# The paged compressed cache laid out by page with contraction elements as rows, gathered page by page and split without transposes

## The chip, the cores and the metric

The kernel runs on one core of a Trainium2 chip. The metric is the device time of one execution in microseconds (us). TensorE is called PE, its weight loads PEld; VectorE is DVE, ScalarE ACT, GpSimd POOL, SyncE SP. SP and POOL issue the DMAs: SP's go through the queue that the profile calls hardware_dynamic (q1), POOL's through software_dynamic (q0), and both run on the same 16 DMA engines.

## The reference

One step of a decoder layer on a prompt of 512 tokens and 8 sample sequences of 4 tokens, with D_MODEL 1024. The change is in the compression of the sample sequences' paged past (1024 rows in 8 pages of 128 for each), and in how x, c and the vectors arrive.

```python
def rmsnorm(x, g):
    xf = x.astype(jnp.float32)
    inv = lax.rsqrt(jnp.mean(xf * xf, axis=-1, keepdims=True) + EPS)
    return (xf * inv).astype(x.dtype) * g

def compress(rows, pe, w1, w2):
    b, t, g, d = rows.shape
    nc = t // CMP_STRIDE
    halves = jnp.pad(rows, ((0, 0), (0, CMP_STRIDE), (0, 0), (0, 0))).reshape(b, nc + 1, CMP_STRIDE, g, d)
    blocks = jnp.concatenate([halves[:, :-1], halves[:, 1:]], axis=2) + pe[:, None, :]
    flat = blocks.transpose(0, 1, 3, 2, 4).reshape(b, nc, g, CMP_BLOCK * d)
    return jax.nn.gelu(flat @ w1) @ w2

def nsa_sample(q, gates, kv_cmp, kv_sel, kv_win, cache_cmp, cache_sel, cache_win, page_table, pe, w1, w2, slopes):
    ...
        rows = cache[page_table].reshape(b, past, 2, N_KV, HEAD_DIM)
    ...
    kc, vc = compress_kv(full_rows(cache_cmp, kv_cmp), pe, w1, w2)
    ...
    mod = jax.nn.silu(c) @ w['w_ada'] + w['b_ada']
    h = rmsnorm(x, w['norm1']) * (1 + sc1) + sh1
```

CMP_STRIDE is 16 and CMP_BLOCK 32, so each block of 32 rows (2048 values of one key or value head) is two halves of 16 rows, and each half is used by two blocks. `w1` is 2048 x 128 for keys and again for values, `w2` 128 x 64.

## The kernel before

All products that need precision are made of three matmuls: each operand is split into a high part (ACT, a copy in the type fp32r) and a low part (DVE, the difference), and hi*hi, lo*hi and hi*lo are summed in PSUM (`mm3`, L222 to L224). Weights come as slabs of 1 MB (`slab`, L208, 128 rows of 8 KB, three buffers with the tag `raw`).

The first stage builds the compressed keys and values of the sample sequences. POOL gathers 1 MB at a time from `cache_cmp` by indices made on DVE from the page table (`cmp_gather`, L466; sixteen gathers, two buffers), DVE copies a gather into order (`cmp_copy`, L476), PE transposes its 128 x 128 pieces against the identity so that the contraction lies on partitions (`cmp_T`, L484), ACT and DVE split the PSUM result (L486, L487), and `cmp_M` (L498 to L500) multiplies by the split `w1`: the moving operand is 512 columns wide, the second half of a block is reached by reading one column further (`c0 = lp * 512 + s`), and one PSUM tile sums a pair of sequences over four gathers. `cmp_finish` (L504 to L514) adds the bias, applies gelu and the second layer. Between these run `mod_slab` 0 to 7 (L269, matmuls of silu(c) with slabs of `w_ada`; `mod_fin`, L280), `phi_split` and `phi_bias` (L440, L441, L447), and in the second half `modulate` (L343 to L345), which makes `h` for the input projection.

Before that stage x arrives as rows and is transposed on PE (L545, L549), its squares are summed by ACT along the row, and c, the vectors and the position table come through small DMAs and small transposes (L577, L580, L585).

After the stage the projection's `linear` calls follow (first `kv_type`), then the attention parts and the feed-forward part; at the end of `modulate` x is stored to `x_dr` (L609) and read back much later.

The order of the instructions of each engine is set when the program is built, by a scheduler that follows the order of the code and moves single instructions ahead where their inputs come earlier. Each engine works its list in order; a wait holds back what stands behind it.

```python
        pool.indirect_dma_start(out=t, out_offset=None, in_=ccv, in_offset=bass.IndirectOffsetOnAxis(ap=ixc[:, col:col + 1], axis=0))
...
                pe.transpose(p[:, g * 128:(g + 1) * 128], g2t[lp][:, v * 4 + g].rearrange("p l d -> p (l d)"), ident)
...
                pe.matmul(po, lhsT=w_h, rhs=mh, start=first, stop=False)
                pe.matmul(po, lhsT=w_l, rhs=mh, start=False, stop=False)
                pe.matmul(po, lhsT=w_h, rhs=ml, start=False, stop=last)
```

## Time and profile before

| what | us |
|---|---|
| median of 3 runs (1332.07 to 1332.87) | 1332.23 |
| the profiled execution, its own time | 1332.59 |
| its span, first to last instruction | 1330.8 |
| first `phi` matmul | 20.22 |
| first `lin` matmul (the compression stage ends) | 161.78 |

The span lies inside the profiled execution's time. A group of instructions in the profile is named by line, engine and operation, then output <- input and the shape, the count, the busy time and the mean time of one in ns, and the idle time before them with what ended it. The busy time of a matmul is the time from its start until its result is out; several are under way at once, so the distance from one start to the next says what one costs in a stream.

### The profile page before, as it was taken

Reading aid. Unit: us, or ns where it says so; the run is one execution under the profiler, and the core shown is the slowest. Engines: PE = TensorE matmul, PEld = TensorE weight load, DVE = VectorE, ACT = ScalarE, POOL = GpSimd, SP = SyncE. Lnnn points to the kernel's source line nnn. Section 1 sums busy time; section 2 is a strip of 40 time slices with the busy share of each in tenths; the row PEclk is TensorE's granted clock in tenths of the full one; section 3 lists DMA queues with packets and bytes.
Section 4 is the critical chain, followed back from the end, with each engine's and each line's share of the span. In section 5 each row is a group of like instructions: output and inputs, shape, how many; then the busy total and the mean of one; then the engine's idle time right before and its main releaser. Section 6 shows DMA issues by size and latency. Waiting matters only on the chain.

```text
span 1330.8 us, 25612 instructions
## 1 busy us (share of the span) xinstructions
PE 1306.2 (98%) x10832; PEld 1206.7 (91%) x10832; DVE 652.3 (49%) x1569; ACT 537.9 (40%) x1065; POOL 69.7 (5%) x123
## 2 busy tenths in 40 slices
PE   7999999999999999999999999999999999999997
PEld 5788899999999988998778778999999999999996
DVE  5549332235455454426677586667333333333335
ACT  6335233433233335226677676345332323222223
POOL 2101030000111110001000000000000000000000
PEclk8999999999999999999999999999999999999999
DMA  9896135763545443834546324431113222122211
GB/s 352 295 329 232 40 113 177 279 225 117 197 179 222 165 159 115 221 119 137 134 143 181 125 91 180 137 127 64 64 64 120 71 90 101 57 88 88 88 65 68
DMA packets 35352, 193.56 MB, mean 145 GB/s; under 512 B 4561, under 2 KB 9945, under 8 KB 17702
## 3 DMA queue, kind: packets, MB, share of 16 engines
q1 hardware_dynamic: 30630, 149.98, 33.4%
q0 software_dynamic: 4608, 41.95, 8.3%
q8 instruction: 85, 1.39, 0.4%
q14 instruction: 29, 0.24, 0.1%
HBM read 174.47 MB, written 25.76 MB: 150 GB/s over the span
## 4 chain that ended last, share of the span: by engine, by line
PE 95%; DMA 2%; DVE 1%; ACT 0%; issue 0%; POOL 0%; POOLq 0%; ACTq 0%; DVEq 0%
PE lin L222 19%; PE lin L223 19%; PE lin L224 19%; PE dn L223 3%; PE dn L222 3%; PE dn L224 3%; PE acc L1162 3%; PE ptp L1168 3%; PE phi L500 2%; PE phi L498 2%; PE phi L499 2%; PE xt L484 2%; PE modp L269 2%; PE kt L879 2%; PE sp L1137 1%; PE sp L1138 1%
## 5 line engine op out<-in xcount | busy, mean ns | idle before, releaser
L222 PE MATMUL lin<-h_hi,wh 128*128 128x288 f32 (+1 forms) x1648 | 478.5, 291 | 0.0
L223 PE MATMUL lin<-h_lo,wh 128*128 128x288 f32 (+1 forms) x1648 | 474.5, 288 | 0.0
L224 PE MATMUL lin<-h_hi,wl 128*128 128x288 f32 (+1 forms) x1648 | 473.2, 287 | 0.0
L222 PEld LDWEIGHTS lin<-h_hi,wh 128*128 128x128 f32 x1648 | 310.5, 188 | 9.4 <-issue 8.1
L223 PEld LDWEIGHTS lin<-h_lo,wh 128*128 128x128 f32 x1648 | 310.0, 188 | 0.5
L224 PEld LDWEIGHTS lin<-h_hi,wl 128*128 128x128 f32 x1648 | 309.4, 188 | 0.3
L218 DVE TENSOR_TENSOR wl<-raw,wh 128x1024 fp32r<-128x1024 f32 (+1 forms) x148 | 178.6, 1207 | 266.1 <-ACT wh L217 265.5
L217 ACT ACTIVATE wh<-raw 128x1024 fp32r<-128x1024 f32 (+1 forms) x148 | 154.9, 1046 | 329.6 <-PE lin L223 236.2
L222 PE MATMUL dn<-f_hi,wh 128*128 128x256 f32 (+1 forms) x352 | 101.9, 289 | 0.0
L223 PE MATMUL dn<-f_lo,wh 128*128 128x256 f32 (+1 forms) x352 | 101.3, 288 | 0.0
L224 PE MATMUL dn<-f_hi,wl 128*128 128x256 f32 (+1 forms) x352 | 101.0, 287 | 0.0
L1144 ACT ACTIVATE P<-P,nms 128x512 f32<-128x512 f32 (+3 forms) x128 | 70.7, 555 | 19.5 <-DVE nms L1143 18.5
L1143 DVE CUSTOM_DVE_ANT_0 P<-sp,ta 128x512 f32<-128x512 f32 (+3 forms) x128 | 57.5, 482 | 29.9 <-PE sp L1131 22.4
L224 PEld LDWEIGHTS dn<-f_hi,wl 128*128 128x128 f32 x352 | 66.3, 188 | 0.0
L222 PEld LDWEIGHTS dn<-f_hi,wh 128*128 128x128 f32 x352 | 66.2, 188 | 0.0
L223 PEld LDWEIGHTS dn<-f_lo,wh 128*128 128x128 f32 x352 | 66.1, 188 | 0.0
L498 PE MATMUL phi<-xh,wph 128*128 128x512 f32 x128 | 53.8, 420 | 0.0
L500 PE MATMUL phi<-xl,wph 128*128 128x512 f32 x128 | 52.0, 408 | 0.0
L499 PE MATMUL phi<-xh,wpl 128*128 128x512 f32 x128 | 51.8, 405 | 0.0
L486 ACT ACTIVATE xh<-xt 128x512 fp32r<-128x512 f32 x64 | 35.0, 597 | 32.6 <-PE xt L484 31.7
L487 DVE TENSOR_TENSOR xl<-xt,xh 128x512 fp32r<-128x512 f32 x64 | 41.1, 684 | 12.9 <-ACT xh L486 12.7
L1168 PEld LDWEIGHTS ptp<-ident,P 128*128 128x128 f32 x320 | 35.7, 141 | 10.9 <-issue 8.9
...
## 6 DMA issues: line engine op xcount, KB each, us to landing
...
out_new_win_sample<-in_cache_win SPq DMA_DIRECT2D x8, 1016.0 KB, 10.8
...
```

What stands on the lines that cost most here:

```text
L217: act.activation(oh, view, AF.Copy)
L218: dve.tensor_sub(ol, view, oh.bitcast(F32))
L222: pe.matmul(p, lhsT=wh[:, k, :], rhs=xh, start=start, stop=False)
L223: pe.matmul(p, lhsT=wh[:, k, :], rhs=xl, start=False, stop=False)
L224: pe.matmul(p, lhsT=wl[:, k, :], rhs=xh, start=False, stop=stop)
L487: dve.tensor_sub(xlb[v][:, lp * 512:lp * 512 + 512], p, xo.bitcast(F32))
L498: pe.matmul(po, lhsT=w_h, rhs=mh, start=first, stop=False)
L499: pe.matmul(po, lhsT=w_l, rhs=mh, start=False, stop=False)
L500: pe.matmul(po, lhsT=w_h, rhs=ml, start=False, stop=last)
L1143: dve.tensor_tensor_reduce(out=t[:, 0:n], in0=sps[br], in1=t_dist[:, 512 - n:512], scale=-hs, scalar=3e38, op0=ALU.add, op1=ALU.min, accum ...
L1144: act.activation(t[:, 0:n], t[:, 0:n], AF.Exp, scale=-1.0, bias=nms[:, c:c + 1], accum_out=sums[:, c:c + 1])
L1168: pe.transpose(tp[:, r * 128:(r + 1) * 128], P[br, r][:, 128 * j:128 * j + 128], ident)
```

## The change

`cache_cmp` arrives in another layout: in each page of 128 positions the 128 rows are now contraction elements (two positions by 64 values), and the columns are key/value, pair of positions, head and block. One gather per page (`cmp_gather`, 64 in all, 128 rows of 2 KB) puts such a page into SBUF as matmuls want it; there are no copies and no transposes. A step `n` of the loop now is one sequence and keys or values. `cmp_split` makes high and low parts from SBUF directly, in two halves of 1024 columns, into the `wh`/`wl` buffers and four `xl` buffers. `cmp_M` does both halves of a block (`s`) as separate 256-column sums, with a moving operand of eight runs of 32 elements; `cmp_finish` shifts and adds the two sums on DVE. The page buffers of sequences 0, 1, 3 and 4 lie where `h` will be, of 2, 5 and 7 in a buffer of their own, of 6 in two slab buffers. x, c and the vectors come transposed (`xT`, `hd`, `hp`), so their transposes go; the squares of x are summed by `square_acc` and `tok_sums`, as in the second norm. `x_dr` goes: x is read a second time from the input. `wake` puts 48 and 36 transposes of the identity, whose result nothing reads, ahead of the stage.

```diff
+    hd = cst.tile([128, HD_W], F32, name="hd")
+    tsm, vec = hd[:, 0:TS_W], hd[:, TS_W:HD_W]
...
-    hh_ = hpool.tile([128, KC, NT], F32R, name="h_hi")
-    hl_ = hpool.tile([128, KC, NT], F32R, name="h_lo")
-    h = (hh_, hl_)
...
-    sync.dma_start(tsm, a["tab_s"])
-        sync.dma_start(t, a["x_prompt"][j * 128:(j + 1) * 128, :])
+    sync.dma_start(hd, a["hd"])
...
+    dve.tensor_scalar(ixc, ptf, 128.0, tsm[:, 51:52], ALU.mult, ALU.add)
...
+    sync.dma_start(hp, a["hp"])
+    peT, w2, c_in = hp[:, 0:64], hp[:, 64:192].rearrange("p (v d) -> p v d", v=2), hp[:, 192:264]
...
-    def cmp_T(v, g2t):
-        for lp in range(2):
-            p = tp_ps(nm("xt"))
-            for g in range(4):
-                pe.transpose(p[:, g * 128:(g + 1) * 128], g2t[lp][:, v * 4 + g].rearrange("p l d -> p (l d)"), ident)
-            xo = xhb[v][:, lp * 512:lp * 512 + 512]
-            act.activation(xo, p, AF.Copy)
-            dve.tensor_sub(xlb[v][:, lp * 512:lp * 512 + 512], p, xo.bitcast(F32))
...
+    def cmp_gather(b):
+        if b == 6:
+            ts = [raw_tile("gt6").rearrange("p (j w) -> p j w", j=4) for _ in range(2)]
+        elif b in (2, 5, 7):
+            ts = [gat.tile([128, 8, 512], F32, tag="gt", bufs=1, name=nm("gt"))]
         else:
+            ts = [hpool.tile([128, KC * NT], F32, tag="h" + "hl"[b in (1, 4)], bufs=1, name=nm("gt"))[:, 0:4096].rearrange("p (j w) -> p j w", j=8)]
+        for pg in range(8):
+            col = b * 8 + pg
+            t = ts[pg // 4][:, pg % 4] if b == 6 else ts[0][:, pg]
+            pool.indirect_dma_start(out=t, out_offset=None, in_=a["cache_cmp"], in_offset=bass.IndirectOffsetOnAxis(ap=ixc[:, col:col + 1], axis=0))
+        gb_[b] = ts
...
+    phi_load(0)
+    cmp_gather(0)
...
+    act.activation(cT[:, :, 0:9], c_in.rearrange("p (k n) -> p k n", k=8), AF.Silu)
+    ada0 = slab("ada", 0)
...
+    def cmp_split(b, v, hc):
+        c0 = v * 256 + hc * 128
+        hi = wpool.tile([128, 8, 128], F32R, tag=("wh", "wl")[hc], bufs=2, name=nm("xh"))
+        lo = gat.tile([128, 8, 128], F32R, tag="xl", bufs=4, name=nm("xl"))
+        n = 8 // len(gb_[b])
+        for q, t in enumerate(gb_[b]):
+            raw, js = t[:, :, c0:c0 + 128], slice(n * q, n * q + n)
+            last_hi[0] = act.activation(hi[:, js], raw, AF.Copy)
+            dve.tensor_sub(lo[:, js], raw, hi[:, js].bitcast(F32))
+        return hi, lo
...
+    def cmp_M(v, xs_, po):
+        for ch in range(8):
+            hi, lo = xs_[ch // 4]
+            c0 = (ch % 4) * 32
+            mh, ml = hi[:, :, c0:c0 + 32], lo[:, :, c0:c0 + 32]
+            for s in range(2):
+                w_h, w_l = wph[v][:, ch + 8 * s, :], wpl[v][:, ch + 8 * s, :]
+                ps_ = po[:, s * 256:s * 256 + 256]
+                pe.matmul(ps_, lhsT=w_h, rhs=mh, start=(ch == 0 and s == 0), stop=False)
+                pe.matmul(ps_, lhsT=w_h, rhs=ml, start=False, stop=False)
+                pe.matmul(ps_, lhsT=w_l, rhs=mh, start=False, stop=(ch == 7 and s == 1))
...
+    def cmp_finish(b, v, po):
+        bp, b2 = b // 2, b % 2
+        pv = po.rearrange("p (s j g c) -> p s g j c", s=2, j=8, g=4)
+        t1 = gat.tile([128, 4, 8, 8], F32, tag="t1", bufs=2, name=nm("t1"))
+        act.activation(t1, pv[:, 0], AF.Identity, bias=pbias[:, v:v + 1])
+        dve.tensor_add(t1[:, :, :, 0:7], t1[:, :, :, 0:7], pv[:, 1, :, :, 1:8])
+        dve.tensor_add(t1[:, :, 0:7, 7], t1[:, :, 0:7, 7], pv[:, 1, :, 1:8, 0])
+        h1 = gat.tile([128, 4, 63], F32, tag="h1", bufs=2, name=nm("h1"))
+        act.activation(h1, t1.rearrange("p g j c -> p g (j c)")[:, :, 0:63], AF.Gelu_apprx_tanh)
+        return lambda: cmp_out2(bp, b2, v, h1)
...
+    def wake(n):
+        p = tp_ps(nm("wake"))
+        for k in range(n):
+            pe.transpose(p[:, (k % 4) * 128:(k % 4) * 128 + 128], ident, ident)
...
+    wake(48)
+    for qt in range(4):
+        phi_split(0, qt)
+    phi_bias(0)
+    cmp_gather(1)
     phi_load(1)
+    sync.dma_start(xT.rearrange("p k n -> p (k n)"), a["xT"])
+    mod_slab(0, ada0)
+    wake(36)
+    accs1 = [xp.tile([128, HW[hf]], F32, name=f"xacc{hf}") for hf in range(2)]
+    fin_, mods = None, []
+    with tc.issue_after(last_m4[0].ins):
+        xs_ = [cmp_split(0, 0, hc) for hc in range(2)]
+    cmp_gather(2)
...
+        po = s_ps(nm("phi"))
+        cmp_M(v, xs_, po)
+        if fin_ is not None:
+            fin_()
+        fin_ = cmp_finish(b, v, po)
+        if n < 15:
+            xs_ = [cmp_split((n + 1) // 2, (n + 1) % 2, hc) for hc in range(2)]
+        if n in (1, 3, 5, 8, 10):
...
+        if 2 <= n < 6:
+            with tc.issue_after(last_hi[0].ins):
+                for k in (2 * n - 4, 2 * n - 3):
+                    for hf in range(2):
+                        square_acc(xT, k, hf, accs1[hf], xp, k == 0)
...
-    sync.dma_start(x1.rearrange("p k n -> p (k n)"), x_dr)
+    sync.dma_start(x1.rearrange("p k n -> p (k n)"), a["xT"])
...
+    cc = f("cache_cmp", 80, 8, 8, 2, 2, 4, 64).transpose(0, 3, 6, 4, 2, 5, 1)
+    arrs["cache_cmp"] = np.ascontiguousarray(cc).reshape(80 * 128, 512)
```

PE, the first instructions of the program before, up to the first `phi` (`xtp` are the transposes of x, `xt` those of the gathered cache):

```order
L545 MATMUL xtp_246<-ident,xr_140 128x128 x4
L545 MATMUL xtp_252<-ident,xr_140 128x128 x4
L549 MATMUL xtp_258<-ident,xs_153 128x32 x8
L484 MATMUL xt_279<-ident,gt_15_273 128x128 x4
L484 MATMUL xt_286<-ident,gt_16_275 128x128 x4
L484 MATMUL xt_293<-ident,gt_15_273 128x128 x4
L484 MATMUL xt_300<-ident,gt_16_275 128x128 x4
L577 MATMUL cp<-ident,xs_153 128x9 x8
L580 MATMUL pep<-ident,perow 128x32
L498 MATMUL phi_307<-xh_172,wph_160 128x512
```

The same place in the changed program, with the semaphores waited for (`pb` is the position bias, `modp` the group of `mod_slab` 0):

```order
L514 MATMUL wake_164<-ident 128x128 x47
L426 MATMUL pb_221<-raw_145,hp 32x128 [waits DMAHW3_49,DMAHW2_49]
L426 MATMUL pb_221<-raw_145,hp 32x128 x15
L430 MATMUL pbt_240<-sel,pbs_238 128x1 [waits DVE_49]
L273 MATMUL modp_255<-raw_161,cT 32x128 [waits DMAHW4_49,Activation_49]
L273 MATMUL modp_255<-raw_161,cT 32x128 x15
L514 MATMUL wake_274<-ident 128x128 x36
L483 MATMUL phi_339<-xh_313,wph_134 128x256 [waits Activation_49]
L484 MATMUL phi_339<-xl_314,wph_134 128x256 [waits DVE_49]
```

One `pb` and one `modp` group stand ahead of the first `phi` now, and no transposes of data.

SP's queue at the start of the program before (`raw` are slabs, `xr` and `xs` the rows of x):

```order
L399 DMA pti<-in_page_table 128x64
L400 DMA tsm<-in_tab_s 128x52
L404 DMA xr_134<-in_x_prompt 128x1024
L404 DMA xr_136<-in_x_prompt 128x1024
L404 DMA xr_138<-in_x_prompt 128x1024
L404 DMA xr_140<-in_x_prompt 128x1024
L418 DMA xs_153<-in_x_sample 32x1024
L419 DMA xs_153<-in_c_prompt 1x1024
L420 DMA xs_153<-in_c_sample 8x1024 [waits DMAHW0_49]
L208 DMA raw_187<-in_wt 128x2048 [waits DMAHW1_49]
```

And in the changed program (the last two waits of slabs are for buffers that weight splits and `mod_slab` 0 set free):

```order
L398 DMA pti<-in_page_table 128x64
L399 DMA hd<-in_hd 128x156
L408 DMA hp<-in_hp 128x264
L210 DMA raw_145<-in_wt 128x2048
L210 DMA raw_161<-in_wt 128x2048
L210 DMA raw_252<-in_wt 128x2048
L523 DMA xT<-in_xT 128x4352
L210 DMA raw_500<-in_wt 128x2048 [waits DMAHW3_49,DVE_49,PE_49]
L210 DMA raw_594<-in_wt 128x2048 [waits DMAHW4_49,DMAHW0_49,PE_49]
L1312 DMA out_new_win_sample<-in_cache_win 16x16256 [waits DMAHW1_49]
```

Three slabs and the whole of xT stand right behind the small tables, where the rows of x stood.

ACT's first split in the changed program names what it waits for: the eight pages of one gather.

```order
L419 ACTIVATE wph_134<-raw_145 128x512 x3
L275 ACTIVATE m_11_272<-modp_255 128x128 [waits PE_49]
L470 ACTIVATE xh_313<-gt_147 128x1024 [waits DMASW4_49,DMASW5_49,DMASW3_49,DMASW6_49,DMASW2_49,DMASW7_49,DMASW1_49,DMASW0_49]
L470 ACTIVATE xh_317<-gt_147 128x1024
L419 ACTIVATE wph_135<-raw_252 128x512 [waits DMAHW5_49]
```

Behind it on ACT stand the other splits and the split of the second `w1` slab.

## Rows read from the trace of the kernel before

**Rows 1.** From the page: the span, the busy time of each engine with its share of the span and its instructions, and the chain that ended last by engine.

```profile
span 1330.8 us, 25612 instructions
...
PE 1306.2 (98%) x10832; PEld 1206.7 (91%) x10832; DVE 652.3 (49%) x1569; ACT 537.9 (40%) x1065; POOL 69.7 (5%) x123
...
PE 95%; DMA 2%; DVE 1%; ACT 0%; issue 0%; POOL 0%; POOLq 0%; ACTq 0%; DVEq 0%
```

**Rows 2.** Busy time by stage: the start, the compression stage from the first `phi` on, and the rest. Columns: the stretch, its length, busy us and instructions of each engine, the granted PE clock (1.00 is full), the DMA engines' busy share and GB/s.

```profile
0.00:20.20 20.20, 10.64 (x65) 9.26 (x65) 8.23 (x24) 14.17 (x24) 6.59 (x17) 0.93 0.88 335
20.20:161.80 141.60, 140.60 (x1043) 112.57 (x1042) 86.40 (x182) 58.18 (x111) 13.22 (x14) 0.99 0.67 246
161.80:1330.80 1169.00, 1154.98 (x9727) 1084.87 (x9726) 557.64 (x1364) 465.50 (x932) 49.88 (x92) 1.00 0.38 130
```

**Rows 3.** All engines in order of time where the compression stage ends. Columns: start, duration, engine, line, operation, and in brackets the idle time before and what ended it.

```profile
159.99 0.68 ACT L504 ACTIVATE h<-phi,pbias 128x504 f32<-128x504 f32 x1 [2.96 <-PE phi L500]
...
160.72 1.13 PE L514 MATMUL ph<-w,h 128*63 128x64 f32 x16 [0.83 <-ACT h L504]
...
161.78 0.40 PE L222 MATMUL lin<-h_hi,wh 128*128 128x288 f32 x1
```

**Rows 4.** PE in order of time, one round of eight transposes and twelve `phi` matmuls late in the stage (the last row's count is cut by the window).

```profile
141.41 1.04 PE L484 MATMUL xt<-ident,gt 128*128 128x128 f32 x8
...
142.52 0.39 PE L499 MATMUL phi<-xh,wpl 128*128 128x512 f32 x1
...
144.87 0.41 PE L500 MATMUL phi<-xl,wph 128*128 128x512 f32 x1
145.11 0.27 PE L484 MATMUL xt<-ident,gt 128*128 128x128 f32 x1
```

**Rows 5.** PE in order of time, the first and the twentieth of a run of 256-column matmuls in the projection.

```profile
203.71 0.28 PE L222 MATMUL lin<-h_hi,wh 128*128 128x256 f32 x1
...
205.94 0.28 PE L223 MATMUL lin<-h_lo,wh 128*128 128x256 f32 x1
```

**Rows 6.** PE in order of time in `cmp_prompt`, where 256 columns in two runs alternate with 128 columns.

```profile
214.00 0.33 PE L675 MATMUL pphi<-px,wph 128*128 128x256 f32 x1
214.17 0.22 PE L676 MATMUL pphi<-px,wpl 128*128 128x128 f32 x1
214.24 0.33 PE L675 MATMUL pphi<-px,wph 128*128 128x256 f32 x1
```

**Rows 7.** PE in order of time: `pb` groups and `modp` groups.

```profile
25.08 1.08 PE L447 MATMUL pb<-raw,peT 128*32 128x128 f32 x32
...
40.52 1.08 PE L269 MATMUL modp<-raw,cT 128*32 128x128 f32 x32
```

**Rows 8.** The first `phi` matmuls on PE in order of time, and the stretch with its granted clock (columns as in Rows 2).

```profile
20.22 0.79 PE L498 MATMUL phi<-xh,wph 128*128 128x512 f32 x1
20.81 0.63 PE L499 MATMUL phi<-xh,wpl 128*128 128x512 f32 x1
21.23 0.63 PE L500 MATMUL phi<-xl,wph 128*128 128x512 f32 x1
...
20.00:25.00 5.00, 5.00 (x16) 3.82 (x14) 4.34 (x9) 4.98 (x9) 1.14 (x1) 0.56 1.02 392
```

**Rows 9.** From the page's costliest groups: the split of a weight of 1024 columns, on DVE and on ACT.

```profile
L218 DVE TENSOR_TENSOR wl<-raw,wh 128x1024 fp32r<-128x1024 f32 (+1 forms) x148 | 178.6, 1207 | 266.1 <-ACT wh L217 265.5
L217 ACT ACTIVATE wh<-raw 128x1024 fp32r<-128x1024 f32 (+1 forms) x148 | 154.9, 1046 | 329.6 <-PE lin L223 236.2
```

**Rows 10.** DVE's groups between 100 and 125 us: the two instructions of `modulate`.

```profile
L343 DVE SCALAR_TENSOR_TENSOR md_u<-xT,A,inv 128x256 f32<-128x256 f32 x14 | 6.3, 476 | 0.0
L345 DVE SCALAR_TENSOR_TENSOR h_lo<-md_u,modT,h_hi 128x256 fp32r<-128x256 f32 x12 | 5.4, 480 | 0.3 <-ACT h_hi L344 0.2
```

**Rows 11.** All engines in order of time at the start: the first two gathers on POOL, and the first use of their data on DVE.

```profile
5.42 1.16 POOL L466 DMA_INDIRECT gt<-in_cache_cmp,ixc  x1 [1.77 <-DVE ixc L412]
...
6.88 0.95 POOL L466 DMA_INDIRECT gt<-in_cache_cmp,ixc  x1 [0.30 <-issue]
...
15.57 1.30 DVE L476 COPY gt<-gt 128x1024 f32<-128x1024 f32 x2 [1.74 <-DMA gt<-in_cache_cmp,ixc]
```

**Rows 12.** DMA queues from 234 to 239 us, where POOL's gather of the sel cache (16 KB rows) and SP's stores of `k_dr` (2 KB rows) are both under way. Columns: packets, MB, share of the 16 engines.

```profile
q0 software_dynamic: 97, 1.59, 88.4%
q1 hardware_dynamic: 96, 0.16, 8.6%
```

**Rows 13.** The stretches 0 to 5 and 15 to 20 us (columns as in Rows 2; the last is GB/s).

```profile
0.00:5.00 5.00, 0.00 (x0) 0.00 (x0) 1.07 (x8) 0.00 (x0) 3.01 (x13) 1.00 0.41 126
...
15.00:20.00 5.00, 3.59 (x24) 3.10 (x25) 3.44 (x6) 4.64 (x7) 0.94 (x1) 0.75 1.03 411
```

**Rows 14.** DMA from 200 to 206 us, where two stores of 256 KB in 2 KB rows are all there is: the GB/s in 40 slices, and one's time from issue to landing; then another such store, from 190 to 200 us.

```profile
GB/s 0 0 0 0 0 0 0 0 0 0 0 0 0 0 0 0 0 0 0 177 382 410 410 314 55 137 369 410 382 369 82 0 0 0 0 0 0 0 0 0
...
k_dr1h<-kh SPq DMA_DIRECT2D x1, 256.0 KB, 2.0
...
k_dr0l<-kl SPq DMA_DIRECT2D x1, 256.0 KB, 2.8
```

**Rows 15.** DMA queues from 77 to 79 us (a cache gather of 8 KB rows and the store of xT, 17 KB rows); columns as in Rows 12.

```profile
q1 hardware_dynamic: 31, 0.45, 53.0%
q0 software_dynamic: 43, 0.35, 41.6%
```

229 lines of the change are left out of this document (60 added, 169 removed).

## The prediction

> **What bounds the kernel now.** I read the page first, then the busy time by stage, then the PE engine's instructions in order of time, then the DMA queues stretch by stretch. The page [rows 1] gives a span of 1330.8 us, PE busy 98% of it and 95% of the chain that ended last. The stages [rows 2] show where PE isn't full: 10.64 of the first 20.20 us, then 140.60 of 141.60 and 1154.98 of 1169.00. The change touches the first two (the compression of the paged cache). From the first `lin` matmul at 161.78 [rows 3] the PE list of the two programs has the same matmuls, but for a handful that change places; those 1169 us I keep. So the question is when that matmul starts. The profiled execution took 1332.59 us, 1.8 over its span and 0.4 over the median of 1332.23; I work from 1332.59.
>
> **The matmuls of the stage.** A 512-column `phi` matmul follows the one before in (144.87 - 142.52) / 10 = 0.235 us [rows 4]; 384 make 90.2 us. A 256-column matmul of the same weights' shape follows in (205.94 - 203.71) / 19 = 0.117 us [rows 5]; the 768 that replace them make 90.1. No gain, no loss, if the new moving operand (8 runs of 32 elements) streams like a plain one. The nearest row is `cmp_prompt`, whose operand has 2 runs of 128: a pair of 256 and 128 columns repeats every 0.24 us [rows 6], as two weight loads of 0.117 would. I take 0; the other reading of these rows is a rival.
>
> **The transposes go.** Eight `xt` and twelve `phi` take 145.11 - 141.41 = 3.70 us [rows 4], the twelve alone 2.82, so eight transposes with the changes of kind cost 0.88. Of 256, 16 run before the first `phi` at 20.22; 240 make 26.4 us, all on PE, which is full there: they count. The DVE copies and the two-engine splitting out of PSUM that fed them were already beside PE; their going is worth 0.
>
> **The rest of PE's stretch.** From 20.22 to 161.78 is 141.6 us. Out: 26.4. Moved ahead of the first `phi`: one `modp` group and one `pb` group, 1.0 each (1.08 until the last result is out) [rows 7], and the small `vp`, 0.2: 2.2. In: five `rmsp` column sums, sixteen second-layer groups in place of eight with their changes of kind, and a longer chain at the end, where the last `phi` is followed by bias, two adds and gelu before `ph` may run; the trace has 0.83 us of waiting there for gelu alone [rows 3], and I add 1.2 for three small instructions. Together 2.4 (estimate; between 1 and 5). Left: 115.4 us, with the slow first matmuls in it: they take 0.4 to 0.6 us apart at a granted clock of 0.56 [rows 8], after PE had been mostly waiting, and will again.
>
> **Beside it.** A step (48 matmuls, 5.6 us) needs two splits of 1024 columns: ACT 2 x 1.046, DVE 2 x 1.207 [rows 9], and about 1 us more each. In four steps `modulate` adds 8 x 0.48 us on DVE [rows 10]: 7.0 against PE's 6.1, a lag of 3.6 us in all. The order has the splits two steps ahead and light steps follow, so I cost it 0; without that cover it is 3.6. The squares, the extra Sqrt table load, the index arithmetic put later and the dropped copy of x to memory have room in the same way: 0.
>
> **The start decides.** Now a step waits for eight page gathers, before for one gather of 1 MB. The trace shows the first issued at 5.42, the next 1.46 us later, data of the first in use at 15.57 [rows 11]. POOL can issue eight by 15. But their data share the 16 DMA engines with SP's queue, and the trace shows how: while 16 KB rows of the sel gather and 2 KB rows of a store are both waiting, 97 packets of one and 96 of the other pass in 5 us, 1.59 MB against 0.16 [rows 12]. The engines alternate by packet, not by byte. Here the gather has the small packets (2 KB rows), and SP has, in the changed order: 0.25 MB of small tables, three slabs of 1.05 MB (8 KB rows), xT of 2.23 MB (17 KB rows), then two more slabs and a 1.04 MB window copy (65 KB rows), which wait only for the first weight split and `mod_slab` 0, done by about 16 us, before xT has drained. Per DMA engine, after the gather's first packet at about 9 us, SP still has some 33 packets, so half of the gather's 64 pass beside them, and half after them. The gather is thus last of nearly all: 8.7 + 2.1 = 10.8 MB at 0.41 MB/us [rows 13] is 26.4 us; data flow from about 3.3 us (0.63 MB by 5 us), and small rows cost about 1: landing at 31. Then one ACT and one DVE split (2.3) and 0.4 for signals: `phi` runs from 33.7. The 36 `wake` transposes end well before and cover nothing.
>
> The rows are not slower for being short: two stores of 256 KB in 2 KB rows move at up to 0.41 MB/us [rows 14].
>
> The stage then ends at 33.7 + 115.4 = 149.1, against 161.78: 12.7 us sooner, 1332.6 - 12.7 = 1319.9. **I say 1320.** The own range of this case is 1314 to 1325 (landing 27 to 34, the 2.4 between 1 and 5).
>
> Later gathers: one element is due every two steps, 13.4 us with `modp`; 2.1 MB of gather, 2.1 of slabs and at most 1.04 of copy are 12.8 us of DMA time. Gather 1 lands at about 39, its step starts at about 50.
>
> **A rule weighed.** The trace shows 256 KB stores landing 2.0 and 2.8 us after issue [rows 14], and two gathers in flight at once [rows 11]. The Trainium skill, "DMA: Bandwidth & Descriptors", section "Rules for kernel authors", asks for at least 1 MiB per DMA for full bandwidth, and its fit gives an estimate of 2.6 us for 256 KB, which the trace's 2.0 and 2.8 bear out. By that, if pages went one by one, 64 would take 166 us and the change would lose; with them in flight together it costs nothing.
>
> **The rivals.**
> (a) The gather gets half of the bytes while both queues wait (0.205 MB/us), or its rows go in groups. For: no row shows POOL's queue with rows as short as 2 KB. Against: [rows 12], and 43 packets of 8 KB against 31, mostly of 17 KB, in 2 us [rows 15]. Then it lands at about 20, limited by POOL, and the time is 1320 - 11 = 1309.
> (b) Slower: the broken moving operand doesn't stream. Place: every `phi`. Taken at their word the starts in [rows 6] give 0.17 us to the 256-column matmul; 768 x 0.052 = 40 us more: 1360. It decides from 12.7 / 768 = 17 ns per matmul on. Against: the pair's sum.
> (c) Slower: the pages land one by one, 2.4 us each (between 2.0 and 2.8) [rows 14]: 64 make 154 us from 5 on, two steps and the end chain after, 175: 1346. From 2.2 us a page on it is a loss. Against: semaphores in eight lanes let eight be in flight.
> (d) The alternation starves the later gathers too: each slab and copy (2.5 us) delays one; four pairs of steps lose 10 us in all: about 1330. For: 12.8 of 13.4 us. Against: three copies only.
>
> **How the numbers follow.** Chances: 0.60 for the forecast, (a) 0.22, (d) 0.08, (b) 0.07, (c) 0.03. The forecast and (a) are faster by over 0.2% (2.7 us, about what a measurement can tell); so is a third of (d), a half of which is within. Faster 0.85, same 0.05, slower 0.10. The range reaches from (a) with some slack, 1306, to (d) just short of no change, 1328; outside lie (b), (c), a little of (a) and (d).
>
> **What would show it.** Right: the first `phi` near 33, PE waiting for the gather by name from about 20; the last page landing after the window copy has drained; `phi` matmuls 0.117 apart; the first `lin` near 149 and 1169 us behind it. Landing at 20 would say (a); `phi` 0.14 or more apart (b); waits for gathers at every second step (c) or (d). Wrong altogether if the 1169 us move.

## The result, and the profile after

The change measured 1348.04 us (median of four, 1343.40 to 1365.41) against 1332.55 for the kernel before on the same chip: a ratio of 1.0104 [1.0058, 1.0151]. One of the four (1365.41) ran in a slower state, and the ratio is that of the other three. I had said 1320 (1306 to 1328): wrong, and on the wrong side. The profiled execution took 1343.92. The page of the changed kernel, its span and its busy times, stands here against [rows 1]:

```profile
span 1342.1 us, 26018 instructions
...
PE 1297.8 (97%) x11020; PEld 1216.4 (91%) x11020; DVE 642.8 (48%) x1554; ACT 540.4 (40%) x1068; POOL 122.4 (9%) x168
```

Busy time by stage, against [rows 2]: up to the first `phi`, up to the first `lin`, and the rest.

```profile
20.20:32.84 12.64, 1.91 (x16) 1.66 (x15) 0.02 (x1) 1.39 (x3) 4.74 (x5) 0.68 1.01 407
32.84:166.08 133.24, 122.50 (x1145) 112.85 (x1145) 79.14 (x177) 68.80 (x128) 55.69 (x52) 0.95 0.58 189
166.08:1342.10 1176.02, 1159.79 (x9728) 1089.80 (x9726) 559.48 (x1365) 465.18 (x931) 49.78 (x92) 0.99 0.39 131
```

Two of my numbers moved. The stage took 133.2 us from first `phi` to first `lin` (I had 116), with PE idle for 10.7 of it; and the part behind, which I had kept at 1169, took 1176.0. PE in order of time where the stage begins and where it ends, against [rows 3]:

```profile
32.84 0.58 PE L483 MATMUL phi<-xh,wph 128*128 128x256 f32 x1 [10.62 <-ACT xh L470]
34.10 0.58 PE L484 MATMUL phi<-xl,wph 128*128 128x256 f32 x1 [0.68 <-DVE xl L471]
...
165.47 0.67 PE L507 MATMUL ph<-hp,h 128*63 128x64 f32 x8 [1.93 <-ACT h L495]
166.08 0.40 PE L224 MATMUL lin<-h_h,wh 128*128 128x288 f32 x1
```

Start and end are as forecast: first `phi` at 32.84 (I had 33), running from 34.1 (33.7), and 1.93 us of waiting at the last `ph` (2.03). The loss lies between. What PE waited for in the stage (us in total, times, longest):

```profile
PE modp L273 <- issue: 3.0, 6, 1.0
PE pbt L430 <- DVE pbs L428: 2.4, 1, 2.4
PE ph L507 <- ACT h L495: 1.9, 1, 1.9
PE phi L483 <- issue: 1.1, 2, 0.7
PE phi L485 <- issue: 0.7, 1, 0.7
...
PE phi L484 <- issue: 0.7, 1, 0.7
```

"issue" means that the profile shows nothing that the engine waited for; "remote", below, that what released it is nothing the profile can name on this core. The same in order of time, PE between 55 and 58.3 us and between 79 and 86 us:

```profile
55.31 0.28 PE L484 MATMUL phi<-xl,wph 128*128 128x256 f32 x1 [0.67 <-issue]
...
56.73 0.28 PE L483 MATMUL phi<-xh,wph 128*128 128x256 f32 x1 [0.67 <-issue]
...
58.17 0.28 PE L485 MATMUL phi<-xh,wpl 128*128 128x256 f32 x1 [0.69 <-issue]
...
79.18 0.64 PE L273 MATMUL modp<-raw,cT 128*32 128x128 f32 x14
80.03 0.39 PE L273 MATMUL modp<-raw,cT 128*32 128x128 f32 x3 [0.21 <-issue]
...
83.62 0.64 PE L273 MATMUL modp<-raw,cT 128*32 128x128 f32 x4 [1.02 <-issue]
...
85.33 0.47 PE L284 MATMUL modq<-ident,m 128*128 128x128 f32 x1
```

A `modp` group that takes 1.0 in [rows 7] takes 85.33 - 79.18 = 6.15. And PE isn't alone; ACT and DVE stand still at the same time, in one piece each, until 58.3:

```profile
58.28 0.28 ACT L275 ACTIVATE m<-modp 128x128 f32<-128x128 f32 x1 [4.35 <-remote]
...
58.31 0.18 DVE L288 TENSOR_TENSOR modT<-modq,hd 128x18 f32<-128x18 f32 x1 [5.52 <-remote]
```

So PE, ACT and DVE are held, for a few us at a time, while POOL goes on issuing gathers in both stretches. 2.4 (`pbt`), 2.5 (`phi` <- issue) and 5.1 (the `modp` group) are 10.0 of the 13 us by which this stage is longer than the undisturbed one below (r_after). Behind the long hold PE's granted clock falls too: 0.77 in 80 to 85 us and 0.54 in 85 to 90.

### The profile page after: what moved, and what is told of

The parts are those of the page before. It is cut to its first block, busy times and chain, and to the rows that moved or that the text cites. A ratio compares the mean times of both kernels' runs of the same rounds, so it can differ in the third digit from the quotient of the medians.

```text
span 1342.1 us, 26018 instructions
## 1 busy us (share of the span) xinstructions
PE 1297.8 (97%) x11020; PEld 1216.4 (91%) x11020; DVE 642.8 (48%) x1554; ACT 540.4 (40%) x1068; POOL 122.4 (9%) x168
## 4 chain that ended last, share of the span: by engine, by line
PE 94%; DMA 2%; DVE 2%; issue 1%; ACT 1%; POOL 0%; another core or an unknown queue 0%; ACTq 0%; DVEq 0%
PE lin L224 19%; PE lin L225 19%; PE lin L226 19%; PE dn L226 3%; PE dn L224 3%; PE dn L225 3%; PE acc L1125 3%; PE ptp L1131 3%; PE phi L483 2%; PE phi L484 2%; PE phi L485 2%; PE modp L273 2%; DMA gt<-in_cache_cmp,ixc 2%; PE kt L842 2%; PE sp L1100 1%
## 5 line engine op out<-in xcount | busy, mean ns | idle before, releaser
L224 PE MATMUL lin<-h_h,wh 128*128 128x288 f32 x976 | 287.2, 294 | 0.0
L226 PE MATMUL lin<-h_h,wl 128*128 128x288 f32 x976 | 281.4, 288 | 0.0
L225 PE MATMUL lin<-h_l,wh 128*128 128x288 f32 x976 | 281.2, 288 | 0.0
L225 PE MATMUL lin<-h_lo,wh 128*128 128x288 f32 (+1 forms) x672 | 193.9, 289 | 0.0
L226 PE MATMUL lin<-h_hi,wl 128*128 128x288 f32 (+1 forms) x672 | 193.4, 289 | 0.0
L224 PEld LDWEIGHTS lin<-h_h,wh 128*128 128x128 f32 x976 | 184.2, 189 | 9.4 <-issue 8.1
L224 PE MATMUL lin<-h_hi,wh 128*128 128x288 f32 (+1 forms) x672 | 192.7, 287 | 0.0
L225 PEld LDWEIGHTS lin<-h_l,wh 128*128 128x128 f32 x976 | 184.1, 189 | 0.4
L226 PEld LDWEIGHTS lin<-h_h,wl 128*128 128x128 f32 x976 | 183.8, 188 | 0.3
L224 PEld LDWEIGHTS lin<-h_hi,wh 128*128 128x128 f32 x672 | 126.8, 189 | 0.0
L483 PE MATMUL phi<-xh,wph 128*128 128x256 f32 x256 | 75.8, 296 | 11.7 <-ACT xh L470 10.6
```

Source lines behind the costliest of these rows:

```text
L224: pe.matmul(p, lhsT=wh[:, k, :], rhs=xh, start=start, stop=False)
L225: pe.matmul(p, lhsT=wh[:, k, :], rhs=xl, start=False, stop=False)
L226: pe.matmul(p, lhsT=wl[:, k, :], rhs=xh, start=False, stop=stop)
L483: pe.matmul(ps_, lhsT=w_h, rhs=mh, start=(ch == 0 and s == 0), stop=False)
```

## The experiments

Theories, from the trace: (S) the one-page gathers, issued back to back on POOL, hold up all engines; rivals (T) it is the traffic of the small rows, (I) the engines wait for their own instructions to be loaded, (P) it is POOL's queue or the number of DMAs, indexed or not. For the later part: (O) the order on ACT, against (W) the window copy standing in SP's queue ahead of `tb`.

The kernels ran on five chips, called A to E here; each ratio is to the kernel before on the same chip (1332.6 to 1333.6 on all five). The last three columns are the first `phi`, the first `lin` and the length of what follows, from the profiled execution. Each chip was used in one session, D in two, so what is said of a chip below could also be the session's. The chip of the first measurement isn't on record.

| kernel | chip | us, median (range) | ratio [95%] | `phi` | `lin` | rest |
|---|---|---|---|---|---|---|
| a_one_seq | A | 1329.62 (1328.29 to 1331.79) | 0.9978 [0.9969, 0.9988] | 32.4 | 151.9 | 1175.8 |
| b_direct_pool | A | 1328.79 (1327.05 to 1331.31) | 0.9972 [0.9962, 0.9982] | 26.7 | 149.3 | 1176.2 |
| c_direct_sp | A | 1330.50 (1328.82 to 1331.94) | 0.9985 [0.9975, 0.9994] | 23.7 | 145.9 | 1184.3 |
| e_no_win | A | 1322.17 (1320.84 to 1323.74) | 0.9925 [0.9909, 0.9942] | 30.6 | 149.4 | 1169.7 |
| r_after | B | 1330.85 (1328.69 to 1332.67) | 0.9983 [0.9974, 0.9992] | 32.8 | 153.0 | 1176.0 |
| g_win_late | B | 1341.79 (1340.76 to 1343.12) | 1.0065 [1.0051, 1.0079] | 30.0 | 150.3 | 1190.6 |
| h_before_win_late | B | 1351.15 (1349.98 to 1353.39) | 1.0141 [1.0125, 1.0156] | - | 160.7 | 1187.5 |
| k_xt_late | B | 1335.48 (1332.85 to 1338.56) | 1.0018 [1.0009, 1.0027] | 25.1 | 144.5 | 1189.8 |
| r_after2 | C | 1345.85 (1344.50 to 1354.29) | 1.0098 [1.0085, 1.0111] | 28.4 | 174.7 | 1177.8 |
| p_plain_operand | C | 1355.43 (1346.24 to 1357.75) | 1.0147 [1.0119, 1.0175] | 29.0 | 176.6 | 1177.9 |
| m1 | C | 1392.61 (1388.01 to 1403.24) | 1.0457 [1.0426, 1.0488] | 43.0 | 164.8 | 1225.6 |
| m2 | C | 1396.88 (1392.44 to 1401.69) | 1.0475 [1.0453, 1.0497] | 43.8 | 173.6 | 1223.8 |
| v1 | D | 1351.58 (1349.83 to 1354.84) | 1.0141 [1.0125, 1.0156] | 42.4 | 172.8 | 1176.9 |
| b2_direct_pool | D | 1329.60 (1326.86 to 1331.57) | 0.9965 [0.9951, 0.9979] | 26.8 | 152.4 | 1177.5 |
| v2 | D | 1335.29 (1332.71 to 1339.40) | 1.0017 [1.0007, 1.0026] | 25.0 | 145.8 | 1190.6 |
| v3 | D | 1358.64 (1357.91 to 1359.54) | 1.0190 [1.0176, 1.0204] | 42.0 | 172.7 | 1184.2 |
| v5 | E | 1330.16 (1329.56 to 1332.78) | 0.9981 [0.9972, 0.9990] | 32.9 | 152.6 | 1175.8 |
| v4 | E | 1321.47 (1320.03 to 1323.13) | 0.9914 [0.9900, 0.9927] | 22.8 | 142.3 | 1177.5 |

**What feeds the stage (a, b, c).** In `cmp_gather`, a lets the later sequences use the first one's pages (put in the buffer that isn't `h`'s):

```diff
     def cmp_gather(b):
+        if b > 0:
+            gb_[b] = gb_[0]
+            return
```

b issues plain DMAs from POOL, one a page, and c nine of 1 or 2 MB from SP; both leave the page table out. The edit of b:

```diff
-            pool.indirect_dma_start(out=t, out_offset=None, in_=a["cache_cmp"], in_offset=bass.IndirectOffsetOnAxis(ap=ixc[:, col:col + 1], axis=0))
+            pool.dma_start(t, a["cache_cmp"][col * 128:col * 128 + 128, :])
```

> Only the first sequence's eight pages are gathered, and all sixteen steps use them (the gathers of the other seven sequences are left out). Theory A (POOL's page gathers, issued eight in a row, hold up signals and instruction starts on every engine) and theory B (the DMA engines, full of short rows, do it, whoever issues them) both say: PE has no waits named issue and no late semaphores between 43 and 90 us, the granted clock doesn't fall after 40 us, phi to first lin takes 115 to 119 us instead of 133.2, and the time falls to about 1327 to 1330, since the 7 us lost later (waiting for px near 322 us) stay. Theory C (the stalls belong to the stream of 256-column matmuls and its instructions, not to the gathers): the stalls stay, 13 us, and the time stays at 1343.

> The 64 page gathers become 64 direct DMAs of the same 256 KB from POOL's queue, without indices (the page table is left out: pages are read in order). Same bytes, same rows, same queue. Theory A, if it is the indices that cost: no stalls on PE, phi to lin 115 to 119 us, time about 1328. Theory A, if it is POOL's writing of descriptors for short rows: the stalls stay, between 5 and 18 us of them, time 1335 to 1350. Theory B: they stay as they are, time 1343.

> The pages come by nine direct DMAs of 1 or 2 MB with 2 KB rows from SP's queue; POOL issues none in the stage (the page table is left out, and since SP has one queue the gathers stand between the slabs in order). Theory A: no waits named issue, none of the late semaphores of 3 to 5 us, no second fall of the clock; the first phi comes near 20 us, since the first 2 MB have only 1.3 MB ahead of them, and the time is about 1315 or less plus any plain wait for a slab behind a gather. Theory B: the same bytes in the same rows stall PE by about as much as before, 8 us or more between 43 and 90 us.

All three came out 2 to 4 us below the kernel before, and in none did PE wait by "issue" in the stage. That looked like (S), but r_after below, with all its indexed gathers, had none on chip B either, so on chip A nothing is told apart. Two things stand: the stage needs 119 to 123 us when it isn't held, and the 7 us behind it are lost with one sequence's gathers as with eight (rest 1175.8 in a). In c the rest is 8 longer still: with the pages in SP's queue its other loads come later (DVE waits 6.6 us for `tb`, `imp` 11.1).

**No window copies (e), later ones (g, h), and the change again (r_after).** e leaves the eight copies of `cache_win` out:

```diff
-        if c2 <= DEC_B:
-            win_shift(c2 - 1)
```

g (from the changed kernel) and h (from the kernel before) put them behind the slabs of the FFN; r_after has no edit:

```diff
         if c2 <= DEC_B:
-            win_shift(c2 - 1)
+            with tc.issue_after(last_slab[0].ins):
+                win_shift(c2 - 1)
```

> The eight window copies are left out, nothing else. Theory on the late part: the 7 us lost after the first lin come from the copy of 1.04 MB that stands ahead of the table tb in SP's queue at 313.8 us; without it imp waits under 1 us, the clock doesn't fall at 325 us, and from the first lin to the end it takes 1169 us again instead of 1176.0. Rival: the later part lost its time to something else in the changed order, and 1176 stays. In the first stage the first phi comes up to 2.5 us earlier (1.04 MB less before the pages have drained) under my accounting by bytes, and not at all if the pages had priority over that copy. The stalls at 43 to 90 us stay under both theories A and B, since the copy at 87 us comes behind them. Time: 1343.9 minus 7 minus 0 to 2.5, 1334 to 1337.

> The changed kernel once more, unaltered. The experiments so far have no stalls named issue on PE, neither with direct DMAs from POOL nor with the indexed gathers but no window copies, so it is open whether the 13 us of stalls belong to the kernel. Theory D (indexed gathers in the company of window copies stall the engines): stalls again, 8 us or more between 43 and 90 us, phi to lin 128 us or more, time 1340 to 1365. Theory E (the stalls belonged to that session: the chip, or where the arrays lay in memory): no stalls, phi to lin 119 to 120 us, and the time is 1343.9 minus 13, about 1330; the 7 us waited for px near 322 us stay under both.

> The window copies are kept, but each stands behind a slab load of the feed-forward part, in the last 250 us. Both theories: first phi about 30.6 as without the copies, no stalls, phi to lin about 119, 1169.7 us behind it, 1322 us, if the feed-forward part has room for 8.3 MB more (its DMA share is 0.2 to 0.3). If it hasn't, up to 8 copies of 2.5 us each are late there: 1342.

> The same in the kernel before. Its copies stood at 25, 46, 101, 104 us and later, and PE there waited for nothing that a copy could have held up, but for 0.7 us at imp and the first 10 us. So no change within 2 us: 1331 to 1333. If the copies cost the kernel before as much as they cost the changed one in the late part, 1325.

r_after is the change undisturbed: 0.9983 [0.9974, 0.9992], 0.17% faster, by my bound of 0.2% no change, and not 1% slower. Its stage and the part behind it:

```profile
32.80:153.00 120.20, 117.46 (x1145) 110.56 (x1145) 78.96 (x177) 68.44 (x128) 62.19 (x52) 0.97 0.61 210
153.00:1329.00 1176.00, 1159.85 (x9728) 1089.90 (x9726) 559.36 (x1365) 464.53 (x931) 49.50 (x92) 0.99 0.39 131
```

and PE's longest wait behind the stage:

```profile
PE imp L814 <- DVE px L811: 3.6, 1, 3.6
```

The stage ends at 153.0 in place of 161.78, 8.8 us sooner, and 7.0 are given back. Without the window copies the rest is 1169.72, as before, and `imp` waits 0.7. The difference is on ACT. Its list in r_after:

```profile
309.34 1.06 ACT L219 ACTIVATE wh<-raw 128x1024 fp32r<-128x1024 f32 x1 [4.95 <-PE lin L225]
310.41 1.28 ACT L808 ACT_TABLE_LOAD   x1
312.02 0.35 ACT L808 ACTIVATE px<-sxs,n 128x63 f32<-128x63 f32 x1 [0.33 <-DVE n L771]
```

and in e_no_win, where the order is that of the kernel before:

```profile
300.01 1.28 ACT L808 ACT_TABLE_LOAD   x1
303.44 0.35 ACT L808 ACTIVATE px<-sxs,n 128x63 f32<-128x63 f32 x1 [2.15 <-DVE n L771]
...
305.30 1.06 ACT L219 ACTIVATE wh<-raw 128x1024 fp32r<-128x1024 f32 x1 [1.42 <-PE lin L225]
```

With the weight split ahead of it, the softmax's exponential (`px`) can't start before PE has freed a weight buffer at 309.3; then comes the table load, and `imp` on PE stands for both. Without it, `px` is done before the buffer is free. The wait is 2.9 us longer than before's 0.7. From `imp` to the end r_after takes 3.0 us longer than the kernel before (1329.1 - 313.05 against 1330.8 - 317.77); the last 1.1 of the 7.0 lie ahead of `imp`, and I haven't separated them. Nearly all of the 3.0 (2.8) is lost in the first 16 us behind `imp`, where the granted clock is low. The stretches 310 to 320 us of r_after (the first with `imp`), and 310 to 315 of e_no_win (`imp` at 306):

```profile
310.00:315.00 5.00, 1.95 (x8) 1.85 (x9) 3.82 (x17) 2.86 (x5) 0.47 (x2) 0.74 0.47 157
315.00:320.00 5.00, 5.00 (x26) 4.85 (x24) 2.61 (x8) 1.19 (x2) 2.35 (x4) 0.58 0.15 64
```

```profile
310.00:315.00 5.00, 5.00 (x42) 3.99 (x42) 3.46 (x12) 1.20 (x2) 2.72 (x4) 1.00 0.38 159
```

PE is full in 315 to 320 but gets through 26 matmuls where an undisturbed 5 us holds 42: the granted clock of 0.58 lies near its lower level (1.2 of 2.4 GHz).

g and h fell the other way. They give before's wait at `imp` (0.7) but no cheap place for the copies: PE's longest waits behind the stage, in g:

```profile
PE lin L224 <- ACT wh L219: 11.5, 6, 1.9
PE lin L226 <- DVE wl L220: 2.4, 5, 0.5
```

The longest of h is the same one (its `lin` for its `wh`: 11.5, 6 times, 1.9): slabs come late in both kernels once the copies are queued among them. I had expected no change from h. In g, 14 of the 21 us by which the later part is longer than e's 1169.7 stand in the two lines shown. In both places that were tried behind the stage the copies cost time: here, and among the kv and q slabs in m1 below.

**xT held (k).** g, with xT's load behind the first pages' split:

```diff
-    sync.dma_start(xT.rearrange("p k n -> p (k n)"), a["xT"])
     mod_slab(0, ada0)
...
         xs_ = [cmp_split(0, 0, hc) for hc in range(2)]
+    dve.tensor_copy(xT[:, 0, 0:1], xs_[0][1][:, 0, 0:1].bitcast(F32))
+    sync.dma_start(xT.rearrange("p k n -> p (k n)"), a["xT"])
```

> As the run before last (window copies late), and xT's 2.23 MB wait on SP until the first pages have been split, where they stood ahead of most of the first gather's data. By my accounting by bytes the last page then lands 2.23 / 0.41 = 5.4 us earlier, at 23.5 to 24.5, first phi 25.2 instead of 30.6, and the time is 1322 - 5.4 = 1316.6. If the pages' data came ahead of xT's anyway, nothing changes: 1322. If POOL's waits for its eight lanes set the landing, up to 2 us of it come: 1320.

The first `phi` came at 25.1 against 30.0 in g: 4.9 us for 2.23 MB, which at 0.41 MB/us are 5.4. So the start goes by bytes, as I reckoned. k is 6.3 us faster than g; against the kernel before, the 20 us of the late copies hide the gain.

**The operand in one run (p), and the change on chip C (r_after2), with two more schedules (m1, m2).** p gives each `phi` matmul a contiguous block of 256 columns, which changes what is computed:

```diff
-            mh, ml = hi[:, :, c0:c0 + 32], lo[:, :, c0:c0 + 32]
+            mh, ml = (z.rearrange("p j c -> p (j c)")[:, c0 * 8:c0 * 8 + 256] for z in (hi, lo))
```

m1 holds xT as k does, with the copies behind kv and q slabs; m2 also holds the phi slab and `mod_slab` 0:

```diff
             sl = slab("kv", ty, v)
+            with tc.issue_after(last_slab[0].ins):
+                win_shift(2 * ty + v)
...
+            if gp == 0:
+                with tc.issue_after(last_slab[0].ins):
+                    win_shift(6 + rp_)
```

```diff
-    phi_load(1)
-    sync.dma_start(xT.rearrange("p k n -> p (k n)"), a["xT"])
-    mod_slab(0, ada0)
...
+    phi_load(1, wpl[0][:, 0, 0:1].bitcast(F32))
...
+    ada0 = slab("ada", 0, hold=xs_[0][1][:, 0, 0:1].bitcast(F32))
```

> The changed kernel, but each phi matmul reads 256 elements in one run instead of eight runs of 32 (this leaves the order of the contraction out: other elements are multiplied, as many of them). In the changed kernel phi matmuls start 0.120 us apart, in the kernel before 256-column ones started 0.117 apart. If the broken operand costs the difference: 0.117, phi to lin 2.2 us shorter, 118.0 instead of 120.2. If not (a weight load each, whatever the operand): 0.120 and 120.2 again.

> The changed kernel a third time, unaltered. When it was first measured it had 13 us of stalls on all engines, the second time none, with the same instructions. If the stalls come only at some times or on some chips: 1329 to 1332 here and no stalls, or, if it strikes again, 1340 and more with waits named issue between 43 and 90 us, in this kernel alone or in the three beside it too.

> Window copies behind the eight slabs that follow the compression (none ahead of the table tb), and xT held on SP until the first pages are split. From the parts measured: first phi 25.1, phi to lin 119.4, 1169.7 behind it, 1.8 around the span: 1316. If the copies delay the slabs of that stretch (DMA share 0.57 there): up to 2.5 us for each of eight, 1316 to 1336.

> As the run before, and the second w1 slab and the first w_ada slab wait too, so that only the tables and one slab stand ahead of the first pages on SP. POOL ends its eighth issue near 14 us. If the pages' landing was set by the bytes around them: it comes near 17, first phi near 20, and with 119.4 and 1169.7 the time is about 1311. If each page needs its 2 us or more and POOL's eight lanes: first phi 22 to 25, 1313 to 1316. If the later arrival of the second slab (needed a step later, 10 us with the slow first matmuls) holds the second step: up to 3 us are given back.

r_after2 is slower than the kernel before, 1.0098 [1.0085, 1.0111], where the same program on chip B was faster: the hold-ups belong to some chips or sessions, and the first measurement (1.0104) is no accident. The times of p, m1 and m2 carry them too and aren't compared with those of other chips. The spacing of `phi` can be read all the same, in a stretch where PE isn't held. Forty-five intervals in r_after2, and as many in p, on the same chip:

```profile
103.35 0.28 PE L485 MATMUL phi<-xh,wpl 128*128 128x256 f32 x1
...
108.74 0.28 PE L485 MATMUL phi<-xh,wpl 128*128 128x256 f32 x1
```

```profile
101.87 0.28 PE L485 MATMUL phi<-xh,wpl 128*128 128x256 f32 x1
...
107.17 0.28 PE L485 MATMUL phi<-xh,wpl 128*128 128x256 f32 x1
```

5.39 / 45 = 0.1198 for the broken operand, 5.30 / 45 = 0.1178 for the plain one: the eight runs cost 2 ns each time, 1.5 us over 768. Rival (b), 52 ns, is dead. m1 and m2 missed by 77 and 86 us. About 18 to 24 of these stand ahead of the first `phi` (43.0 and 43.8, where I had 25.1 and 20), and 10 more in m2's stage; 54 to 56 are behind the stage and have a reason of their own, in m1:

```profile
PE lin L224 <- ACT wh L219: 41.1, 6, 14.3
```

v1 below holds xT in the same way and has 1176.9 there, so it is the new place of the copies. That a copy held behind one slab holds the slab after it on the same queue is my reading of it.

**Indexed or direct (v1, b2, then v2, v3).** v1 is the changed kernel with xT held, seven copies behind xT and the eighth behind `tb` and `stT`; b2 is b again, on the chip of v1:

```diff
-    sync.dma_start(stT.rearrange("p k n -> p (k n)"), a["state_conv"])
+    st_dma = sync.dma_start(stT.rearrange("p k n -> p (k n)"), a["state_conv"])
+    with tc.issue_after(st_dma.ins):
+        win_shift(DEC_B - 1)
...
-        if c2 <= DEC_B:
-            win_shift(c2 - 1)
+        if c2 < DEC_B:
+            with tc.issue_after(xt_dma.ins):
+                win_shift(c2 - 1)
```

v2 gathers by a direct DMA whose address is read from the page table into a POOL register; it holds xT, puts the copies behind it as in v1, and lets ACT's queue load `tb` and `stT`. v3 is v2 with the indexed gather back, and no other difference:

```diff
-            pool.indirect_dma_start(out=t, out_offset=None, in_=a["cache_cmp"], in_offset=bass.IndirectOffsetOnAxis(ap=ixc[:, col:col + 1], axis=0))
+            pv = pool.value_load(pti[0:1, col:col + 1], min_val=0, max_val=N_PHYS - 1)
+            pool.dma_start(t, a["cache_cmp"][bass.ds(pv * 128, 128), :])
...
-    sync.dma_start(tb, a["tab_b"])
+    act.dma_start(tb, a["tab_b"])
```

> The changed kernel with three edits in SP's queue: xT waits until the first pages are split, seven window copies stand behind xT where the order puts them, the eighth behind the table tb. Where the stalls don't strike: first phi 25.1, phi to lin 119.4 to 120.2, imp waits under 1 us and 1169.7 from the first lin on, 1316 in all. If the copies in the kv and q stretch cost what they cost before (nothing seen but the one ahead of tb): no more; if their new places hold a slab: up to 2.5 us each. Where the stalls strike: 13 to 25 us on top, 1330 to 1341.

> The 64 direct page DMAs from POOL's queue again, now beside a kernel with the indexed gathers. If the kernel beside it stalls: indices to blame (theory A, first form) means none here, phi to lin under 123 us, 1327 to 1331; POOL's descriptors or the traffic to blame (theory A, second form, or B) means stalls of 8 us or more here too, 1338 or more. If the kernel beside it doesn't stall, 1327 to 1331 under all theories, and the question stays open.

> A version that computes everything: each page comes by a direct DMA from POOL's queue whose page number POOL reads from the page table into a register (no index list); xT waits until the first pages are split; the window copies stand behind xT; the table tb and the conv state come by ACT's queue, so that no copy stands ahead of them. From the parts measured: first phi at most 25.1, since the direct DMAs brought it at 26.7 even behind xT; phi to lin 119.4 to 123, no stalls anywhere; imp under 1 us and 1169.7 behind the first lin; 1311 to 1320. If reading a register holds POOL for 1 us or more per page, the first phi comes later, up to 28, and 1319 to 1323. If a copy beside tb on the same DMA engines delays it as much as one ahead of it: 7 more.

> The run before with the indexed gathers in place of the register-addressed DMAs, and no other difference. If the indices are what holds the engines up: on a chip where it strikes, stalls here and none in the run beside it, 13 us or more between the two times; where it doesn't strike, both the same within 3 us. If any stall were POOL's or the pages' traffic, both kernels would have it.

v3 is 1358.64 and v2 1335.29: 23 us from the indexed form alone, on one chip in one session. At the first `lin` v3 is even 26.9 us later (172.65 - 145.76); 6.4 of them v2 loses behind the stage. The stage of v2 and then of v3 (columns as above):

```profile
25.00:145.76 120.76, 117.94 (x1145) 111.00 (x1145) 79.19 (x178) 68.38 (x128) 28.35 (x53) 0.97 0.64 237
```

```profile
41.97:172.65 130.68, 119.42 (x1146) 110.92 (x1145) 76.67 (x177) 66.77 (x126) 54.24 (x43) 0.96 0.56 197
```

and PE's longest waits from 20 us to the end of the stage, of v2 and then of v3:

```profile
PE phi L484 <- ACT xh L471: 4.2, 1, 4.2
```

```profile
PE wake L514 <- issue: 12.8, 11, 2.2
PE ph L503 <- ACT h L495: 7.5, 1, 7.5
```

Two different things are in these lines. Ahead of the first `phi` the engines are held: even the `wake` transposes, which wait for no data, stand for 12.8 us, and ACT stands for 26 us before an instruction whose input PE had ready at 18.8. The 7.5 us at `ph` are something else, a plain wait for pages: ACT's split of the last sequence, which stands ahead of what `ph` needs, waits 13.02 us for its gather by name, and two of that gather's issues took 5.83 and 3.50 us on POOL. ACT and POOL in v3:

```profile
38.64 0.28 ACT L275 ACTIVATE m<-modp 128x128 f32<-128x128 f32 x1 [26.17 <-remote]
...
150.79 1.06 ACT L470 ACTIVATE xh<-gt 128x1024 fp32r<-128x1024 f32 x1 [13.02 <-DMA gt<-in_cache_cmp,ixc]
```

```profile
130.86 5.83 POOL L448 DMA_INDIRECT gt<-in_cache_cmp,ixc  x1 [0.30 <-issue]
137.00 3.50 POOL L448 DMA_INDIRECT gt<-in_cache_cmp,ixc  x1 [0.30 <-issue]
```

So 17.0 of the 26.9 us are lost ahead of the first `phi`, and 7.5 of the 9.9 in the stage to late pages (v1 and p have the same wait, 9.2 and 9.6). Bytes, rows, queue and number of DMAs are the same in v2 (5120 packets, 16.78 MB in POOL's queue up to 175 us in both), and neither happens there: (T) and (P) fall. (I) has little left for PE: it runs the same matmuls in both, two `modp` groups a few places apart. What is left is (S), and of it the indexed form. The pair v1 and b2 says the same a second time (22 us), though there xT, the copies and the page table differ too; b2's one wait in the stage, 2.6 us at `pbt`, is behind a split on DVE that waits for a page by name. The indexed form alone isn't enough, though: the kernel before has sixteen indexed gathers of 1 MB, and takes 1332.6 us on C and 1333.2 to 1333.6 on D. What POOL did, first in v2, then in v3:

```profile
60.14 0.54 POOL L449 DMA_DIRECT2D gt<-in_cache_cmp  x1 [4.37 <-DVE modT L289]
61.31 0.54 POOL L449 DMA_DIRECT2D gt<-in_cache_cmp  x1 [0.64 <-issue]
```

```profile
64.61 0.95 POOL L448 DMA_INDIRECT gt<-in_cache_cmp,ixc  x1 [0.30 <-issue]
65.86 1.14 POOL L448 DMA_INDIRECT gt<-in_cache_cmp,ixc  x1 [0.30 <-issue]
```

v2's gain in the stage was lost behind it: PE waits 9.1 us for one weight split, whose slab stood behind stores in SP's queue, and 6.3 at `imp`.

**A version that beats both (v5, v4).** v5 is the changed kernel with v2's direct gather and v1's place for the eighth copy, the others where the change has them; v4 holds xT as well. Both compute everything.

> The changed kernel with two edits: each page comes by a direct DMA from POOL whose page number is read from the page table into a register, and the eighth window copy stands behind the table tb in SP's queue. SP's order is otherwise that of the changed kernel. From the parts: first phi 26.7 as with the direct DMAs, phi to lin 120 to 125.6, no stalls wherever it runs, imp waits 1 us and 1169.7 behind the first lin, 1.8 around: 1318 to 1324. If the indices weren't the cause, stalls and 1335 or more on the chips that show them; if the copy weren't, 7 more: 1325 to 1331.

> The run before, and xT waits until the first pages are split; a window copy of 1.04 MB takes its place ahead of the pages, so 2.23 - 1.04 = 1.19 MB less stand beside them: first phi 2.9 us earlier, 23.8, and 2.9 us less in all, 1315 to 1321. If the landing is set by POOL's issues (the eighth ends at 15.2) and not by the bytes: no change from the run before.

v4 takes 1321.47, 0.9914 [0.9900, 0.9927]. Its first `phi`:

```profile
22.75 0.39 PE L484 MATMUL phi<-xh,wph 128*128 128x256 f32 x1 [2.89 <-ACT xh L471]
```

10.2 us ahead of v5's 32.9, twice what xT's bytes explain. The rest is on SP, which works its list in order: the slabs behind the held xT wait with it. SP in v5, then in v4:

```profile
12.56 1.96 SPq L210 DMA_DIRECT2D raw<-in_wt  x2
```

```profile
25.70 6.86 SPq L210 DMA_DIRECT2D raw<-in_wt  x3
```

xT and two slabs are 2.23 + 2.10 = 4.33 MB less beside the first pages, which at 0.41 MB/us are 10.6. v5 settles (W): the copy stands behind `tb` there, and the later part still takes 1175.8, with ACT's order as in r_after. In v4 the wait at `imp` (3.3) and the 1177.5 behind the stage are still there: with e's order there would be about 7 us more to have, an estimate from e's 1169.7 that no run tested. That v4 is free of hold-ups was seen on chip E alone; whether the indexed form is held there was not tried.

## Why the prediction was wrong, point by point

The profiled execution's 1343.92 is, to 0.1, the 1319.9 of the sum and 13.0 of hold-ups, 7.0 behind the stage and 3.9 in the start and the stage.

- **"Those 1169 us I keep": failed.** It took 7 us more or a little over, in every run of the change that has no other schedule behind the stage (1175.8 to 1177.9). I looked only at PE's list, in which a handful of matmuls change places. What decides is ACT's: one weight split went ahead of `px`, `imp` waits 3.6 in place of 0.7, and the clock falls behind it. With before's order `imp` waits 0.7 (e and g, and v1, which has its copies ahead of `tb` but for the last; v1's 1176.9 are lost elsewhere, with 2.6 of waits for weight splits near 283 us); with the new one (r_after, v5) 3.3 to 3.6, wherever the last copy stands. No run changed that order by itself, so it is the best explanation and not shown alone.
- **"Left: 115.4 us": mis-sized.** From running `phi` to `lin` r_after takes 153.0 - 34.06 = 118.9, 3.5 more. 768 x (0.1198 - 0.1174) = 1.8 of it is the spacing, which I had put at nothing; the other 1.7 lie in the sum of what comes in, 2.4, for which I gave 1 to 5. Which part of it is larger I haven't separated. With 0.4 for the start, this is the whole 3.9 between 149.1 and 153.0.
- **"Later gathers": failed, by the part that I didn't price.** That they land in time is right for the change itself: behind the first, PE waits for no page at any step of r_after or of the first profile. But I counted only their bytes, and put what their issue does to the other engines at nothing. On some chips or sessions PE, ACT and DVE are held while they are issued: 13 us in the first profile, 17 ahead of the first `phi` in v3, where the last pages come late besides. Neither can be read from the trace of before, whose sixteen gathers have rows of 8 KB and hold nothing up.
- **The start: right in the number, and in the main in the mechanism.** First `phi` 32.80 and 32.84 for 33; k, e and v4 confirm the accounting by bytes (e: 2.2 us for 1.04 MB less, which are 2.5). It isn't all: in b the same bytes are under way, but the first page is issued at 1.61 us in place of 4.59, and the first `phi` comes 6.1 us earlier. And the sum's 1 for small rows and 0.4 for signals come from no row; that they fit is partly luck.
- **The transposes and the halves of `phi`: right.** 0.120 a matmul, PE full in the stage; the end chain 1.92 for 2.03.
- **Rivals:** (a) did not come: the gather was last, as predicted. (b) is 1.5 us, not 40. (c) and (d): no gather was late for PE in the change as it was measured; in v1, v3 and p, where the engines are held, the last sequence's pages were. The Trainium skill ("DMA: Bandwidth & Descriptors", section "Rules for kernel authors") asks for at least 1 MiB per DMA for full bandwidth. I had weighed that 64 pages of 256 KB would lose if they went one by one. They don't: v4 loads 64 of them, and its stage takes 119.6 us with no wait of PE for a page behind the first; no run measures the bandwidth of such pages by themselves.

Undisturbed, the sum is 161.78 - 153.0 = 8.8 won and 7.0 lost: 1.8 us, 1330.85. The 3.9 alone would have left 1323.8, inside my range; with the 7.0 it is 1330.8, past the 1328; the first profile's other 13 are the hold-ups.
